# Output map of a hybrid encoder layer: seven block products with sums, or plain quarters with the feed-forward sums made per token tile

## Chip, cores and metric

One core of a Trainium2 chip runs the whole kernel. The metric is the device time of one execution in microseconds (us). The engines are PE (TensorE; PEld is its weight load), DVE (VectorE), ACT (ScalarE), POOL (GpSimd) and SP (SyncE, which issues most DMAs here).

## What is computed

One encoder layer on 1024 tokens of width 1024, all in float32, and a final norm:

```python
u = rms_norm(h, norm_mix[l])
proj = u @ w_in[l]
...
merged = jax.nn.sigmoid(g_pool) * y_pool + jax.nn.sigmoid(g_attn) * y_attn
h = h + merged @ w_out[l]
u = rms_norm(h, norm_ffn[l])
h = h + (jax.nn.silu(u @ w_ffn_gate[l]) * (u @ w_ffn_up[l])) @ w_ffn_down[l]
...
return rms_norm(h, norm_final)
```

`y_pool` and `y_attn` are two token mixers (pooling windows, and windowed attention), each followed by a map to width 1024, which the text calls a branch. `w_out` is the output map; gate, up and down have an inner width of 2816.

## The kernel before

**Arithmetic.** A float32 operand is split into two parts that PE takes (type fp32r): `hi` is ACT's cast of it, and `lo` is operand minus `hi`, made on DVE or POOL (`split`, L81). A product of two operands is three matmuls: hi by hi, hi by lo, lo by hi. A matmul covers 128 rows of the contraction and 512 columns.

**Seven products for eight.** Most maps are done by a scheme that cuts both operands in 2 x 2 blocks and computes seven block products in place of eight, from sums and differences of blocks. For gate and up the blocks of the activations are A11, A12 (first 512 tokens, first and second half of the width) and A21, A22 (last 512 tokens), and the sums are S1 = A21 + A22, S2 = S1 - A11, S3 = A11 - A21, S4 = A12 - S2. Products P1 and P2 need A11 and A12 alone; P5 needs S1, P6 S2, P7 S3, P3 S4, P4 A22 (`A_OF`, L126). The weight differences are made on POOL (`less`, L140).

**Weights.** All weight chunks come through one queue in the order of use (`specs`, `ahead`, `weights`): a 512 KB load into one of four `raw` tiles, then a split into one of four `whi` and one of four `wlo` tiles. A chunk is 12 matmuls of PE work.

**Stages around the change.** (1) The branch of the attention is mapped, gated and added to `merged`, first for token half 0, then for half 1 (`branch_step`, L687; its operand comes back from `a_dram` through `load_branch`, L564, into `a_hi`, `a_lo`). `merged` is kept transposed, [width, tokens], in two halves. (2) The output map `merged @ w_out` runs in the seven-product scheme (`operands_of`, L751; `block_products`, L809; `wo_done`, L909). Its P1 and P2 need only token half 0 and stand between the two branch halves; P5, P7, P6, P3, P4 follow half 1. Sums of `merged` blocks are made on DVE, weight differences on POOL, and results are added to rows `o`, which hold x. (3) The second norm takes rows tile by tile (`second_norm`, L885), and `finish` (L892) transposes a tile on PE (`tp`) and writes it to `merged`, whose place is free by then; for the first 512 tokens it also makes A11 and A12. (4) The first products of gate and up run (P1 and P2 of the first four column pairs), and meanwhile `u_block` (L970) makes A22, S1, S2, S3, S4 one after the other over 512 tokens, with the sums of S2 and S4 on POOL. Then gate and up continue to the end, and the down map follows.

**Order.** A scheduler puts each engine's instructions in an order when the program is built, so the order on an engine is not the order of the code. Each engine, and the SP queue of DMA issues, then works strictly in that order. Tiles of a pool that is opened after another was released may lie in the same memory, and then wait for its last users.

Of the kernel before, what the change touches and what calls it, by code (L numbers as in the profile page):

```python
# [8 lines left out]
F32 = mybir.dt.float32  # L9
# [5 lines left out]
P = 128  # L15
# [39 lines left out]
def encoder_kernel(ctx, tc, x, norm_mix, w_in, w_pool_group, pool_scale, sink, w_pool_branch,  # L55
# [788 lines left out]
    for name in ("A11", "A12"):  # L844
        combos[name] = tuple(first.tile([P, 4, HALF], F32R, name="%s_%s" % (name, s)) for s in ("hi", "lo"))
    op = tc.alloc_tile_pool(name="op", bufs=1)
    gain2 = const.tile([P, D], F32, tag="gain", bufs=1, name="gain_ffn")
    nc.scalar.dma_start(out=gain2, in_=norm_ffn[0:1, :].partition_broadcast(P))
    WO_ORDER = ("P1", "P2", "P5", "P7", "P6", "P3", "P4")
    NO = KT // 2  # L850
    _, wo_operands = operands_of(w_out, (range(NO), range(NO, KT)), NO,
                                 lambda i, r, k: merged[r][:, NO * i + k], [op],
                                 lambda prod, k: nc.vector if WO_POOL[prod] <= k else nc.gpsimd)

    def queue_wo(products):
# [36 lines left out]
    def finish():  # L892

        u2, t = pend.pop(0)
        ts = slice((t % 4) * P, (t % 4 + 1) * P)

        def emit(b, pv):
            m = merged[t // 4][:, 4 * b:4 * b + 4, ts]
            nc.scalar.copy(out=m, in_=pv)
            if t < 4:  # L900
                hi, lo = combos["A1%d" % (b + 1)]
                if LO_POOL[b]:
                    split(m, hi[:, :, ts], lo[:, :, ts], eng=nc.gpsimd)
                else:
                    split(pv, hi[:, :, ts], lo[:, :, ts])

        transposed(u2, emit)

    def wo_done(prod, t, ps):  # L909
        if prod == "P1":  # L910
            nc.scalar.copy(out=p1[t], in_=ps)
        elif prod == "P2":
            nc.scalar.copy(out=p2[t], in_=ps)
        elif prod == "P5":
            add_to(4 + t, 1, ps)
            add_to(t, 1, ps)
        elif prod == "P7":
            add_to(4 + t, 1, ps)
        elif prod == "P6":
# [11 lines left out]
    def wo_after(prod, t):  # L931
        if prod == "P4":
            finish()
            if t + U2_BUFS < NT // 2:
                second_norm(t + U2_BUFS)
# [292 lines left out]
```

## Time and profile before

| what | us |
|---|---|
| median of 3 runs (lowest to highest) | 1240.76 (1240.11 to 1240.97) |
| the profiled execution's own time | 1242.44 |
| span of the profile, first to last instruction | 1240.7 |
| PE busy | 1173.0 |
| DVE busy | 869.3 |
| POOL busy | 648.4 |
| ACT busy | 552.9 |

The profiled execution took 1.7 us more than the median and 1.7 us more than its span. Matmuls are pipelined: the end of one overlaps the start of the next, so the pace is read from the distance between starts. The granted clock (PEclk) is the share of full TensorE speed in a stretch. A wait is put down to the instruction whose end released it.

### The profile page before, as it was taken

To read this page: it belongs to the slowest core of one execution; us is meant where nothing else is said; L and a number is where in the kernel's file an instruction comes from. 1 tells how busy PE (TensorE), PEld (TensorE's weight loads), DVE (VectorE), ACT (ScalarE), POOL (GpSimd) and SP (SyncE) were. 2 spreads that over 40 slices of the span, in tenths; PEclk is the share of its full clock that TensorE was granted. 3 is DMA by queue.
4 is the path that set the end of the run, shared out by engine and by line. 5 is a ranking of instruction groups with operands and counts; after the bars stand their busy time and mean duration, and the time that the engine had idled before them with its cause. 6 is when DMAs were issued, how large, how long until landed. Compare 5 with 4: busy or idle time off the path is not lost.

```text
span 1240.7 us, 15495 instructions
## 1 busy us (share of the span) xinstructions
PE 1173.0 (95%) x5236; PEld 955.4 (77%) x5236; DVE 869.3 (70%) x1257; ACT 552.9 (45%) x1064; POOL 648.4 (52%) x531
## 2 busy tenths in 40 slices
PE   7899999999999998798699999999999999999996
PEld 5688888887778885576488888888888878887775
DVE  6954785757899656996996555665555675789974
ACT  6633354536677552357433333333333344443453
POOL 5833453344545638957765454654445623179530
PEclk9999999999899999799899999999999999999998
DMA  6343133126421654624144223232233358876362
GB/s 204 111 133 122 60 110 119 53 86 215 139 80 46 214 161 143 233 96 160 34 143 130 77 78 117 90 116 94 77 110 102 110 195 297 300 251 238 118 212 110
DMA packets 112337, 170.10 MB, mean 137 GB/s; under 512 B 7617, under 2 KB 63937, under 8 KB 112258
## 3 DMA queue, kind: packets, MB, share of 16 engines
q1 hardware_dynamic: 104338, 142.64, 35.3%
q0 software_dynamic: 6480, 21.24, 4.8%
q10 hardware_dynamic: 1440, 5.24, 1.1%
q8 instruction: 41, 0.67, 0.2%
q14 instruction: 38, 0.31, 0.1%
HBM read 128.99 MB, written 40.11 MB: 136 GB/s over the span
## 4 chain that ended last, share of the span: by engine, by line
PE 77%; DVE 14%; issue 3%; DMA 2%; POOL 2%; ACT 1%; SPq 0%; POOLq 0%; DVEq 0%; ACTq 0%
PE dn L820 17%; PE Y L179 16%; PE X L179 15%; PE Z L179 13%; PE W L179 8%; DVE wlo L84 2%; DVE o L870 2%; DVE al L84 1%; PE br L211 1%; PE br L210 1%; PE br L212 1%; DVE S_lo L84 1%; PE pt L657 1%; PE pv L670 1%; PE pv L671 1%
## 5 line engine op out<-in xcount | busy, mean ns | idle before, releaser
L83 ACT CAST whi<-raw 128x512 fp32r<-128x512 f32 x344 | 212.1, 620 | 392.9 <-PE Y L179 86.2
L84 DVE TENSOR_TENSOR wlo<-raw,whi 128x512 fp32r<-128x512 f32 x304 | 267.6, 889 | 73.7 <-ACT whi L83 73.0
L140 POOL TENSOR_TENSOR raw<-raw 128x512 f32<-128x512 f32 x140 | 196.6, 1406 | 217.5 <-DVE wlo L84 188.8
L820 PE MATMUL dn<-wlo,ah 128*128 128x512 f32 x420 | 167.8, 400 | 11.2 <-DVE wlo L84 11.0
L820 PE MATMUL dn<-whi,ah 128*128 128x512 f32 x420 | 159.6, 397 | 8.5 <-ACT ah L83 5.3
L820 PE MATMUL dn<-whi,al 128*128 128x512 f32 x420 | 162.4, 397 | 1.7 <-DVE al L84 1.7
L179 PE MATMUL X<-S_lo,whi 128*128 128x512 f32 x280 | 109.9, 393 | 4.1 <-DVE S_lo L84 4.0
L179 PE MATMUL X<-S_hi,whi 128*128 128x512 f32 x280 | 109.9, 392 | 2.7 <-ACT whi L83 2.7
L179 PE MATMUL X<-S_hi,wlo 128*128 128x512 f32 x280 | 109.4, 391 | 0.0
L820 PEld LDWEIGHTS dn<-wlo,ah 128*128 128x128 f32 x420 | 80.9, 193 | 31.6 <-DVE wlo L84 14.3
L820 PEld LDWEIGHTS dn<-whi,ah 128*128 128x128 f32 x420 | 80.2, 191 | 28.0 <-ACT ah L83 7.1
L820 PEld LDWEIGHTS dn<-whi,al 128*128 128x128 f32 x420 | 80.7, 192 | 19.3 <-DVE al L84 2.6
L84 DVE TENSOR_TENSOR al<-ab,ah 128x512 fp32r<-128x512 f32 x69 | 68.1, 987 | 31.1 <-ACT ah L83 30.8
L83 ACT CAST ah<-ab 128x512 fp32r<-128x512 f32 x69 | 42.7, 618 | 78.2 <-PE dn L820 76.5
L179 PE MATMUL Z<-A_hi,whi 128*128 128x512 f32 x176 | 70.0, 399 | 1.9 <-ACT A_hi L83 1.9
L179 PE MATMUL Z<-a,whi 128*128 128x512 f32 (+1 forms) x240 | 70.2, 377 | 0.3 <-ACT a L83 0.3
L179 PE MATMUL Z<-A_lo,whi 128*128 128x512 f32 x176 | 70.0, 398 | 0.0
L179 PE MATMUL Z<-A_hi,wlo 128*128 128x512 f32 x176 | 69.6, 396 | 0.0
L84 POOL TENSOR_TENSOR wlo<-raw,whi 128x512 fp32r<-128x512 f32 x40 | 56.8, 1425 | 23.2 <-ACT whi L83 20.0
L179 PEld LDWEIGHTS X<-S_lo,whi 128*128 128x128 f32 x280 | 52.7, 188 | 16.7 <-DVE S_lo L84 5.2
L179 PEld LDWEIGHTS X<-S_hi,whi 128*128 128x128 f32 x280 | 52.6, 188 | 15.1 <-ACT whi L83 3.3
L647 POOL TENSOR_SCALAR s<-s,den 128x384 f32<-128x384 f32 (+1 forms) x32 | 38.7, 1219 | 46.7 <-DVE den L645 27.5
(262 smaller groups left out, 2759.5 us busy)
## 6 DMA issues: line engine op xcount, KB each, us to landing
raw<-in_w_ffn_down_dram SPq DMA_DIRECT2D x45, 512.0 KB, 5.5
ab<-act_dram SPq DMA_DIRECT2D x31, 512.0 KB, 5.5
raw<-in_w_in_dram SPq DMA_DIRECT2D x26, 512.0 KB, 3.9
raw<-in_w_ffn_gate_dram SPq DMA_DIRECT2D x22, 512.0 KB, 4.1
raw<-in_w_ffn_up_dram SPq DMA_DIRECT2D x22, 512.0 KB, 3.8
act_dram<-sums POOLq DMA_DIRECT2D x44, 256.0 KB, 2.8
raw<-in_w_out_dram SPq DMA_DIRECT2D x18, 512.0 KB, 4.4
sg<-g_dram SPq DMA_DIRECT2D x32, 256.0 KB, 3.3
```

The source lines that it names most:

```text
L83: ins = nc.scalar.copy(out=hi, in_=src)
L84: (eng or nc.vector).tensor_tensor(out=lo, in0=src, in1=as32(hi), op=ALU.subtract)
L140: nc.gpsimd.tensor_tensor(out=out, in0=x0, in1=x1, op=ALU.subtract)
L179: nc.tensor.matmul(ps, wt[:, c], at[:, k, cols], start=opening and k == 0 and i == 0, stop=k == 3 and i == 2, skip_group_check=not opening)
L210: nc.tensor.matmul(ps, wh, xh, start=first, stop=False)
L211: nc.tensor.matmul(ps, wh, xl, start=False, stop=False)
L212: nc.tensor.matmul(ps, wl, xh, start=False, stop=last)
L647: (nc.gpsimd if i in POOL_HEADS else nc.vector).tensor_scalar(out=s[:, i, :W], in0=s[:, i, :W], scalar1=den[:, i:i + 1], scalar2=None, op0 ...
L657: nc.tensor.transpose(out=ps[:, i * P:(i + 1) * P], in_=s[:, i, jj * P:(jj + 1) * P], identity=ident)
L670: nc.tensor.matmul(ps, v, pt[jj][0], start=jj == 0, stop=False)
L820: nc.tensor.matmul(ps[t], at[:, ts], wt, start=opening and k == 0 and e == 0, stop=k == nk - 1 and e == 2, skip_group_check=not opening)
L870: (eng or nc.vector).tensor_tensor(out=o[t][:, half_of(c)], in0=src, in1=o[t][:, half_of(c)], op=ALU.add)
```

## The change

**What it does.** The output map is computed in plain quarters: token half by output half, eight contraction chunks each (`wo_product`), with 384 matmuls instead of 336. `merged` is split once per half into `m_hi`, `m_lo` (`split_merged`: half 0 beside branch half 1, half 1 after it). The weight chunks of `w_out` need no differences, and all quarters come after both branch halves. A quarter's last three chunks (`WO_TAIL`) are held back and run row by row, so that rows finish one after the other. The tiles of the first 512 tokens are normed and transposed beside the third quarter (`first_half`). For the last 512 tokens, `emit_sums` makes A22, S1, S2, S3 of one 128-token tile directly behind its transposes, all sums on DVE, in the memory of the split of `merged`; S4 alone remains a block over 512 tokens (`last_block`), also on DVE. The `lo` parts of the first gate and up chunks and of all `w_out` chunks move from POOL to DVE. By the instruction orders POOL has 58 instructions fewer and the DVE count falls by 6. Loads of `w_out` go from 18 to 16. Up to the output map a line of the changed kernel has a number 4 lower than before (L84 is L80).

```diff
+    def split_merged(half):
+        for j in range(KT):
+            split(merged[half][:, j], *[m[:, j] for m in m_split[half]])
...
+        def emit_sums(b, pv):
+
+            a11 = merged[0][:, :4, ts]
+            a21, s = [merged[1][:, 4 * i:4 * i + 4, ts] for i in range(2)]
+            if b == 0:
+                nc.scalar.copy(out=a21, in_=pv)
+                return
+            nc.vector.tensor_tensor(out=s, in0=pv, in1=a21, op=ALU.add)
+            split(pv, *part("A22"))
+            split(s, *part("S1"))
+            nc.vector.tensor_tensor(out=s, in0=s, in1=a11, op=ALU.subtract)
+            split(s, *part("S2"))
+            nc.vector.tensor_tensor(out=a21, in0=a11, in1=a21, op=ALU.subtract)
+            split(a21, *part("S3"))
...
-    wo_products(WO_ORDER[:2])
     while pool_steps:
         branch_step()
     brs[0].release()
     early = tc.alloc_tile_pool(name="early", bufs=1, side="right")
+    open_split()
+    split_merged(1)
...
+    def wo_product(half, c, beside):
+
+        ps = [bank("wo%d" % t) for t in range(4)]
+        hi, lo = m_split[half]
+
+        def accumulate(k, t, w):
+            ts = slice(t * P, (t + 1) * P)
+            for e, (at, wt) in enumerate(((hi, w[0]), (lo, w[0]), (hi, w[1]))):
+                nc.tensor.matmul(ps[t], at[:, k, ts], wt, start=k == 0 and e == 0, stop=k == KT - 1 and e == 2)
+
+        for k in range(KT - WO_TAIL):
+            w = weights()
+            for t in range(4):
+                accumulate(k, t, w)
+            ahead(1)
+            beside(k)
+        tail = [weights() for _ in range(WO_TAIL)]
+        for t in range(4):
+            for i in range(WO_TAIL):
+                accumulate(KT - WO_TAIL + i, t, tail[i])
+            row = 4 * half + t
+            if row not in o:
+                o[row] = ot.tile([P, D], F32, tag="o", bufs=4, name="o")
+                nc.sync.dma_start(out=o[row], in_=x[row * P:(row + 1) * P, :])
+            add_to(row, c, ps[t])
+            square(row, c, ot)
+            if c and t < U2_BUFS:
+                second_norm(row)
+        ahead(WO_TAIL)
...
-        if unit[2] == 1 and not late_pools:
-            open_late()
-            u_block("A22")
-            u_block("S1")
-            made |= set(("A22", "S1"))
-        if name not in made:
-            u_block(name)
-            made.add(name)
+        if (unit, prod) == f_seq[4 * EARLY + 2]:
+            last_block()
```

**SP queue, end of the attention.** `at` tiles are stored to `a_dram`, `sg` are gate loads, and `raw<-a_dram` are the two parts of the operand of branch half 1. Before:

```order
L679 DMA a_dram_70<-at_4138 128x2x128
L574 DMA sg_4240<-g_dram_67 128x512
L763 DMA raw_4378<-in_w_out_dram 128x2x512
L574 DMA sg_4265<-g_dram_67 128x512
L679 DMA a_dram_70<-at_4193 128x2x128
L574 DMA sg_4476<-g_dram_67 128x512
L100 DMA raw_4424<-in_w_attn_branch_dram 128x4x256
L574 DMA sg_4497<-g_dram_67 128x512
L574 DMA sg_4520<-g_dram_67 128x512
L100 DMA raw_4458<-in_w_attn_branch_dram 128x4x256
L574 DMA sg_4541<-g_dram_67 128x512
L568 DMA raw_4468<-a_dram_70 128x2x512
```

With the change:

```order
L564 DMA raw_4298<-a_dram_70 128x2x512
L570 DMA sg_4215<-g_dram_67 128x512
L675 DMA a_dram_70<-at_4138 128x2x128
L570 DMA sg_4238<-g_dram_67 128x512
L570 DMA sg_4259<-g_dram_67 128x512
L570 DMA sg_4306<-g_dram_67 128x512
L675 DMA a_dram_70<-at_4193 128x2x128
L564 DMA raw_4302<-a_dram_70 128x2x512
```

The last store (`at_4193`) moves behind one more gate load, the third after the store before it, and the second part of the operand is loaded directly behind that store.

**DVE, the same place.** `al` and `m_lo` are lo parts of `merged`, `a_lo` that of the operand of branch half 1; each `sg` is the product with a gate. Before:

```order
L711 TENSOR_TENSOR sg_4240<-br_4242,sg_4240 128x512
L84 TENSOR_TENSOR al_4317<-merged_2675,ah_4316 128x512
L84 TENSOR_TENSOR wlo_4289<-raw_4282,whi_4288 128x512
L711 TENSOR_TENSOR sg_4265<-br_4267,sg_4265 128x512
L84 TENSOR_TENSOR wlo_4321<-raw_4282,whi_4320 128x512
L84 TENSOR_TENSOR al_4339<-merged_2675,ah_4338 128x512
```

With the change:

```order
L80 TENSOR_TENSOR m_lo_4214<-merged_2675,m_hi_4213 128x512 x3
L707 TENSOR_TENSOR sg_4238<-br_4240,sg_4238 128x512
L80 TENSOR_TENSOR m_lo_4214<-merged_2675,m_hi_4213 128x512 x3
L80 TENSOR_TENSOR wlo_4279<-raw_4276,whi_4278 128x512
L707 TENSOR_TENSOR sg_4259<-br_4261,sg_4259 128x512
L80 TENSOR_TENSOR a_lo_3997<-raw_4302,a_hi_3996 128x2x512
```

The second `a_lo` of branch half 1 now stands behind six `m_lo`, and its load has no products of the output map beside it.

**DVE, behind the second norm.** Before, the sums over 512 tokens of S1 (L977) and S3 (L982), and their `lo` parts:

```order
L977 TENSOR_TENSOR merged_2676<-merged_2676 128x512
L84 TENSOR_TENSOR S1_lo_5487<-merged_2676,S1_hi_5486 128x512
L84 TENSOR_TENSOR wlo_5561<-raw_5555,whi_5560 128x512
L982 TENSOR_TENSOR merged_2676<-merged_2675,merged_2676 128x512
L84 TENSOR_TENSOR S3_lo_5491<-merged_2676,S3_hi_5490 128x512
L84 TENSOR_TENSOR S1_lo_5487<-merged_2676,S1_hi_5486 128x512
L84 TENSOR_TENSOR wlo_5584<-raw_5578,whi_5583 128x512
```

With the change, for the last token tiles (L933, L936, L938 are the sums of a tile; each `wlo` is of a weight chunk):

```order
L933 TENSOR_TENSOR merged_2676<-tp_5395,merged_2676 128x4x128
L80 TENSOR_TENSOR A22_5250<-tp_5353,A22_5250 128x4x128
L80 TENSOR_TENSOR S1_5251<-merged_2676,S1_5251 128x4x128
L80 TENSOR_TENSOR wlo_5459<-raw_5456,whi_5458 128x512
L80 TENSOR_TENSOR S2_5252<-merged_2676,S2_5252 128x4x128
L80 TENSOR_TENSOR S3_5253<-merged_2676,S3_5253 128x4x128
L80 TENSOR_TENSOR wlo_5483<-raw_5477,whi_5482 128x512
L938 TENSOR_TENSOR merged_2676<-merged_2675,merged_2676 128x4x128
L80 TENSOR_TENSOR A22_5250<-tp_5395,A22_5250 128x4x128
L936 TENSOR_TENSOR merged_2676<-merged_2676,merged_2675 128x4x128
L80 TENSOR_TENSOR S1_5251<-merged_2676,S1_5251 128x4x128
```

The sums start with the first transposed tile instead of after the last, and the last S1 part, which the first P5 product needs, comes behind the sums of the three tiles before it.

## Rows read from the trace of the kernel before

**Rows 1.** The page: span and busy time.

```profile
span 1240.7 us, 15495 instructions
PE 1173.0 (95%) x5236; PEld 955.4 (77%) x5236; DVE 869.3 (70%) x1257; ACT 552.9 (45%) x1064; POOL 648.4 (52%) x531
```

**Rows 2.** Windows: length, busy (count) of PE, PEld, DVE, ACT, POOL; PEclk, DMA share, GB/s.

```profile
482.50:523.00 40.50, 27.98 (x97) 20.81 (x97) 40.40 (x33) 15.09 (x30) 33.96 (x22) 0.83 0.55 208
523.00:562.00 39.00, 36.24 (x157) 29.08 (x157) 36.52 (x48) 15.66 (x35) 26.02 (x19) 0.96 0.27 89
562.00:570.50 8.50, 3.75 (x26) 2.94 (x26) 7.60 (x11) 7.84 (x18) 5.47 (x6) 1.00 0.67 243
570.50:594.60 24.10, 21.37 (x97) 17.09 (x97) 14.03 (x16) 16.41 (x32) 16.17 (x13) 0.93 0.40 123
594.60:622.00 27.40, 19.68 (x68) 14.51 (x69) 27.40 (x23) 12.20 (x22) 22.43 (x14) 0.88 0.05 17
```

**Rows 3.** Waits of PE, 482.5 to 622 us: total, times, longest.

```profile
PE dn L820 <- DVE wlo L84: 5.2, 1, 5.2
PE X L179 <- DVE S_lo L84: 4.0, 2, 2.7
```

**Rows 4.** Timeline of PE: start, duration, instruction, idle before.

```profile
438.13 0.39 PE L820 MATMUL dn<-whi,ah 128*128 128x512 f32 x1
...
459.91 0.39 PE L210 MATMUL br<-a_hi,whi 128*128 128x512 f32 x1
...
495.15 0.80 PE L820 MATMUL dn<-whi,ah 128*128 128x512 f32 x1 [2.80 <-ACT ah L83]
...
497.45 0.63 PE L820 MATMUL dn<-wlo,ah 128*128 128x512 f32 x1
497.88 0.63 PE L820 MATMUL dn<-whi,ah 128*128 128x512 f32 x1
...
567.07 1.20 PE L239 MATMUL tp<-ident,u 128*128 128x128 f32 x9 [0.81 <-ACT merged L899]
...
619.11 0.78 PE L179 MATMUL W<-S_lo,whi 128*128 128x512 f32 x1
```

**Rows 5.** Timeline of DVE and POOL near 595 us.

```profile
593.86 0.68 DVE L982 TENSOR_TENSOR merged<-merged 128x512 f32<-128x512 f32 x1
594.46 0.68 DVE L977 TENSOR_TENSOR merged<-merged 128x512 f32<-128x512 f32 x1
595.07 1.78 DVE L84 TENSOR_TENSOR S_lo<-merged,S_hi 128x512 fp32r<-128x512 f32 x1
...
594.48 1.82 POOL L140 TENSOR_TENSOR raw<-raw 128x512 f32<-128x512 f32 x1 [2.29 <-DMA raw<-in_w_ffn_up_dram]
```

**Rows 6.** Groups, 482 to 700 us: xcount | busy us, mean ns | idle before.

```profile
L84 DVE TENSOR_TENSOR S_lo<-merged,S_hi 128x512 fp32r<-128x512 f32 x16 | 20.0, 1291 | 0.0
L889 DVE SCALAR_TENSOR_TENSOR u<-o,rstd,gain_ffn 128x1024 f32<-128x1024 f32 x8 | 14.3, 1804 | 2.5 <-POOL rstd L882 2.5
```

**Rows 7.** Timeline of the SP queue: a gate load of branch half 1.

```profile
432.22 0.33 SPq L574 DMA_DIRECT2D sg<-g_dram  x1
```

**Rows 8.** DMA issues: count, KB each, median us to landing.

```profile
raw<-a_dram SPq DMA_DIRECT2D x4, 512.0 KB, 4.0
a_dram<-at SPq DMA_DIRECT2D x16, 128.0 KB, 1.8
```

**Rows 9.** Groups, 438 to 482 us.

```profile
L84 DVE TENSOR_TENSOR wlo<-raw,whi 128x512 fp32r<-128x512 f32 x10 | 8.2, 839 | 1.0 <-ACT whi L83 1.0
L711 DVE TENSOR_TENSOR sg<-br,sg 128x512 f32<-128x512 f32 x7 | 4.8, 690 | 8.7 <-PE br L212 7.5 <-issue 1.3
L84 DVE TENSOR_TENSOR a_lo<-raw,a_hi 128x1024 fp32r<-128x1024 f32 x2 | 2.5, 1226 | 7.7 <-ACT a_hi L83 7.7
L83 ACT CAST a_hi<-raw 128x1024 fp32r<-128x1024 f32 x2 | 2.1, 1050 | 4.4 <-DMA raw<-a_dram 4.4
```

**Rows 10.** The page, costliest groups: weight differences on POOL.

```profile
L140 POOL TENSOR_TENSOR raw<-raw 128x512 f32<-128x512 f32 x140 | 196.6, 1406 | 217.5 <-DVE wlo L84 188.8
```

More of the change, by code (lines that the diff above doesn't have):

```diff
@@ L895, in finish, with part @@
         ts = slice((t % 4) * P, (t % 4 + 1) * P)
+        def part(name):
+            hi, lo = combos[name]
+            return hi[:, :, ts], lo[:, :, ts]
         def emit(b, pv):
-            m = merged[t // 4][:, 4 * b:4 * b + 4, ts]
+            m = merged[0][:, 4 * b:4 * b + 4, ts]
             nc.scalar.copy(out=m, in_=pv)
[L900 to L905, printed above, removed]
@@ L931, in wo_after @@
[L931 to L935, printed above, removed]
-        elif t < U2_BUFS:
-            second_norm(t)
+            if LO_POOL[b]:
+                split(m, *part("A1%d" % (b + 1)), eng=nc.gpsimd)
+            else:
+                split(pv, *part("A1%d" % (b + 1)))
+        def emit_sums(b, pv):
[11 more added lines that the diff above has]
+            split(a21, *part("S3"))
@@ L945, in encoder_kernel @@
     f_seq = [(("f", m_, j), p) for m_, j, p in f_seq]
[L946 to L953 removed]
+    queue_products(f_seq, lambda u: ((w_g, w_u)[u[1]], 2 * u[2] * P), f_kinds)
     while pool_steps:
@@ L957, in encoder_kernel @@
     early = tc.alloc_tile_pool(name="early", bufs=1, side="right")
+    open_split()
+    split_merged(1)
     ot = tc.alloc_tile_pool(name="ot", bufs=1)
-    for t in range(NT):
-        o.append(ot.tile([P, D], F32, tag="o", bufs=NT, name="o"))
-        nc.sync.dma_start(out=o[t], in_=x[t * P:(t + 1) * P, :])
     ssq = ot.tile([P, 2, NT], F32, name="ssq2")
-    for t in range(NT // 2):
-        add_to(t, 0, p2[t], nc.gpsimd)
-        square(t, 0, ot)
-    wo_products(WO_ORDER[2:])
-    for t in range(U2_BUFS):
-        second_norm(4 + t)
@@ new lines, in first_half, with last_block @@
+    def first_half(k):
+        if k < NT // 2:
+            finish()
+            if k + U2_BUFS < NT // 2:
+                second_norm(k + U2_BUFS)
+    for half in range(2):
+        for c in range(2):
+            wo_product(half, c, first_half if (half, c) == (1, 0) else lambda k: None)
+    for half, names in enumerate((("A22", "S1"), ("S2", "S3"))):
+        for name in names:
+            in_place_of_split(half, name)
+    def last_block():
+        for k in range(4):
+            hi, lo = (t[:, k] for t in combos["S4"])
+            s = merged[1][:, 4 + k]
+            nc.vector.tensor_tensor(out=s, in0=merged[0][:, 4 + k], in1=s, op=ALU.subtract)
@@ L1067, in open_late @@
         ot.release()
-        op.release()
         second = tc.alloc_tile_pool(name="second", bufs=1)
-        for name in ("S1", "S2", "S3", "S4", "A22"):
-            combos[name] = tuple(second.tile([P, 4, HALF], F32R, name="%s_%s" % (name, s)) for s in ("hi", "lo"))
+        combos["S4"] = tuple(second.tile([P, 4, HALF], F32R, name="S4_%s" % s) for s in ("hi", "lo"))
         late_pools.extend((second, tc.alloc_tile_pool(name="ff", bufs=1)))
@@ L1113, in sums_of @@
             spill(name, j, out)
-    made = set(("A11", "A12"))
     for i, (unit, prod) in enumerate(f_seq):
```

87 lines of the change are left out of this document (27 added, 60 removed).

## Prediction

> **What bounds the kernel now.** The page comes first: PE is busy 1173.0 of 1240.7 us, DVE 869.3, POOL 648.4 [rows 1]. So PE sets the end, and the question is where its 67.7 idle us lie and where it runs slowly. The view by window answers the first part. From 482.5 us (end of the branch) to 622 us (first products of gate and up that need sums) PE is busy 27.98 + 36.24 + 3.75 + 21.37 + 19.68 = 109.0 of 139.5 us; 30.5 us are idle, while DVE is busy all the time at both ends of the stretch (40.40 of 40.50 and 27.40 of 27.40) and POOL for 33.96 and 22.43 [rows 2]. The waits of PE name the releasers: DVE and ACT, with parts of weights and of sums [rows 3]. The timeline gives the second part. Between 438.13 and 459.91 us 96 matmuls start 0.227 us apart; after a wait, as at 495.15, they start 0.43 us apart and last 0.63 us, the pace of the lower clock, 1.2 GHz in place of 2.4 [rows 4]. From 495.15 to 619.11 I count 56 such matmuls, in six runs, each soon after a wait; the granted clock of the windows with the longest waits is 0.83 and 0.88 [rows 2, 4]. They cost 56 x 0.20 = 11.2 us. Of what PE loses in this stretch, 30.5 + 11.2 = 41.7 us, the change can get back all or part, since nothing in it remains as it was.
>
> **What goes.** The operands of P5, P7, P6, P3 and P4, made one chunk ahead from sums on DVE and differences on POOL, are gone; `w_out` chunks are loaded and split only. With them go the waits from 482.5 to 562 us. The transposes of the first 512 tokens move beside the third quarter, those of the last 512 beside the first products of gate and up, so PE has other work between them. Removed: 41.7 us.
>
> **What is added on PE.** 384 matmuls for 336: 48 x 0.227 = 10.9 us, all on the path. The 64 transposes stay.
>
> **What hides the rest.** In the quarters PE eats a chunk in 12 x 0.227 = 2.7 us. A chunk needs one cast and one `wlo` (0.84 us on DVE [rows 9]) and half a load; the adds, squares, stores and norms of a quarter are spread over 21.8 us. The casts of `m_hi`, the 16 `m_lo` and the `lo` parts that leave POOL are priced at nothing where PE works on ready operands; their cover is the branch (22 us) for half 0 and two quarters (43 us) for half 1. POOL is left with powers and a few `lo` parts. The x loads (four at first, four more when rows are free) and the `h_dram` stores sit on the SP queue between `w_out` loads, and eight chunks are loaded or split ahead, 21.8 us of cover.
>
> **New wait 1, at 438 us.** Before, the products P1 and P2 of the output map, 21.8 us, stood between the branch halves and hid the return of the attention's last part. Now half 1 follows at once, and its seventh matmul needs the second part of its operand at 438.13 + 7 x 0.23 = 439.7 us. The last store to `a_dram` now stands on SP behind a gate load that was issued at 432.22 [rows 7], so it goes at 432.6, lands 1.8 later, and the part lands 4.0 after that [rows 8]: 438.4. Cast and `lo`, 1.05 and 1.23 us [rows 9], end at 440.7: a wait of 1.0 us. But DVE has six `m_lo`, a `wlo` and two gate products ahead of that `lo`, and the memory of `m_hi` is that of the stored tile, so they start after the store has landed, at 434.4 + 0.6 = 435.0: 7 x 0.84 + 2 x 0.69 = 7.3 us [rows 9], then 1.23, which ends at 443.5 and makes a wait of 3.8. If each of the seven met POOL's gate sums and took 1.78 us, as a `lo` part does beside POOL [rows 5], the wait would be 10.7. I take 4, since 0.84 is the mean beside the same POOL work; 1.0 and 10.7 are the ends.
>
> **New wait 2, behind the second norm.** From the first gate product to the first product with S1, PE has 96 matmuls and 32 transposes: 96 x 0.227 + 32 x 1.20 / 9 = 26.0 us [rows 4]. By the order of instructions DVE has in that time 24 short instructions with both inputs in SBUF (sums, `lo` parts, weights), 9 that read PSUM and 3 of the norm; up to the last part of S4 17 more, and one that reads PSUM, against three product pairs, 3 x 5.45 = 16.3 us. Alone, DVE starts one every 0.60 us, also with two SBUF inputs; beside a POOL subtraction the same kind takes 1.78 [rows 5]. With a mean m for these 41, and 1.80 for a norm [rows 6], the wait is 24m + 9 x 0.60 + 3 x 1.80 - 26.0 + 17m + 0.6 - 16.3 = 41m - 30.9. At m = 0.60 it is nothing. In the last window POOL was busy for 22.43 of 27.40 us, 0.82 [rows 2], and the mean of a `lo` part of a sum was 1.29 [rows 6], 0.61 above its 0.68 alone. Now POOL has only ten weight differences there, 10 x 1.41 us [rows 10] in some 42 us, 0.33. So m = 0.60 + 0.61 x 0.33 / 0.82 = 0.85, and the wait is 4 us. The ends are 0 and, at 1.29, 22.
>
> The Trainium skill, SBUF — State Buffer, "Who interferes with whom", states that a VectorE instruction with two SBUF inputs and a GpSimd instruction that reads SBUF exclude each other for a whole instruction. The trace agrees with the direction (0.68 alone, 1.78 beside POOL [rows 5]). By that rule each of the ten differences would hold DVE up for its full 1.41 us: 41 x 0.60 + 14.1 - 30.9 = 7.8 us, and the forecast would be 1224, inside its own range, so this is no rival.
>
> **New wait 3, the clock.** A wait of some us is followed by 56 / 6, about nine, slow matmuls [rows 4], 1.9 us. I take one such run.
>
> **Sum.** -41.7 + 10.9 + 4 + 4 + 2 = -20.8 us. The profiled execution took 1242.44 us, of which 1.7 lie outside the span; it would come to 1221.6. Its time is 1.7 above the median, 1240.76, on which the forecast is **1220.0**.
>
> **The rivals.** (A) *Nothing new waits*, beyond the 1.0 us of the load: -41.7 + 10.9 + 1.0 = -29.8, 1211. For it: DVE alone keeps ahead of PE, and POOL may do its differences early. Against it: the order of DVE puts the S1 part of the last tile behind nearly all sums of the others. (B) *VectorE half blocked behind the second norm*: m = 1.29 as now gives 22 in place of 4, 1238; m = 1.1 gives 14, 1230. For it: the same kinds of instruction had that mean in the trace. Against it: half of the POOL work of that window, the sums of S2 and S4 and weight parts, is gone. (C) *Slower*: the same place, but every one of the 41 loses to POOL and takes 1.78: 41 x 1.78 - 30.9 = 42 us, 1258. It decides from 41m - 30.9 = 30.8 - 6, m = 1.36, just above the mean now. For it, POOL's ten differences would have to be spread so that each instruction meets one; against it, ten cannot meet 41 unless each is stretched. The rule on exclusion above would make it likelier only with more POOL work than there is. (D) *The quarters do not run at full pace*: a wait for weights at each of the 32 chunks, 0.65 us each, takes back the 20.8 us, about the same time as before. For it: PE was idle for 40.50 - 27.98 = 12.5 us in the first window of the output map [rows 2]; against it: its operands there were sums and differences, which are gone.
>
> **How the numbers follow.** The forecast's case, 1214 to 1228, takes new wait 1 between 1 and 8 us and wait 2 up to 10: 0.67. A, below 1214: 0.11. B, 1228 to 1238: 0.13. C: 0.06. D: 0.03. A measurement tells 0.2%, 2.5 us, from no change. Faster: 0.67 + 0.11 + 0.13 = 0.91; same: D, 0.03; slower: C, 0.06. The range 1210 to 1233 takes in A and the nearer half of B and leaves out some 0.17.
>
> **What would show it.** Right: PE's idle time from the end of the branch to the S4 products under 13 us, against 30.5; 384 matmuls of the output map 0.227 us apart with a granted clock near 1.00; a wait of 1 to 8 us some seven matmuls into branch half 1, on `a_lo`; a mean of S1 and S3 parts on DVE under 1.0 us; PE waiting on S parts for 0 to 10 us. Wrong: waits on `whi` or `wlo` inside the quarters, waits of transposes on `u`, S parts above 1.3 us, or a clock below 0.9 in the quarters.

## The result and the profile after

| what | before, us | after, us |
|---|---|---|
| median (lowest to highest), same chip | 1240.43 (1237.14 to 1240.97) | 1207.78 (1206.62 to 1211.03) |
| ratio of the medians, 95% interval | | 0.9746, 0.9721 to 0.9772 |
| the profiled execution's own time | 1242.44 | 1207.96 |
| PE waits from 430 to 640 us | 30.5 | 3.3 |
| first branch product with attention weights to first product of the down map | 600.60 | 571.03 |
| first to last product of the down map | 218.81 | 215.57 |

The change is worth 32.65 us. The forecast was 20.8 us less, 1220.0, and its range began at 1210: the direction was right, the gain larger than the range allowed. The last two rows of the table are starts of PE's instructions in its timeline, 409.88, 1010.48 and 1229.29 us before, 408.21, 979.24 and 1194.81 after. The first of these stretches holds everything that the change touches: before it and behind it the traces of the two kernels have the same instructions in the same order on every engine. It is called *the stretch* below.

The page of the changed kernel, span and busy time (before: [rows 1]):

```profile
span 1206.2 us, 15486 instructions
PE 1167.2 (97%) x5284; PEld 955.4 (79%) x5284; DVE 834.1 (69%) x1251; ACT 543.1 (45%) x1044; POOL 563.8 (47%) x473
```

PE has 48 matmuls more and is busy for 5.8 us less, mainly since none of its work in the stretch runs at the lower pace any more. The view by window, with the columns of [rows 2], shows it for branch half 1 and what is around it, the four quarters, the first products of gate and up, and the first ones that need sums:

```profile
438.00:465.00 27.00, 26.15 (x111) 20.15 (x110) 27.00 (x31) 11.74 (x21) 15.64 (x9) 1.00 0.62 210
465.00:553.00 88.00, 88.00 (x410) 73.21 (x409) 45.02 (x66) 39.59 (x81) 11.37 (x11) 1.00 0.48 170
553.00:578.00 25.00, 24.70 (x121) 20.32 (x120) 25.00 (x37) 17.98 (x33) 10.73 (x8) 1.00 0.52 162
578.00:605.00 27.00, 25.97 (x113) 20.89 (x113) 24.99 (x32) 9.96 (x18) 11.41 (x9) 1.00 0.27 86
```

In the quarters PE has no gap in 88 us and DVE only half a load (45.02 of 88.00). Behind the norm DVE is full (25.00 of 25.00), and yet PE stands idle for 0.30 us there and for 1.03 us in the next window. The granted clock is 1.00 in all four, where [rows 2] has 0.83, 0.96, 1.00, 0.93 and 0.88 for the windows of before. These are all of PE's waits between 430 and 640 us (total, times, longest), against the 30.5 us of which [rows 3] shows two. `W`, `X`, `Y` and `Z` are results of gate and up products, `br` those of the branch; `S` stands for the parts of S1, S2 and S3, whose `hi` comes from ACT and whose `lo` from DVE:

```profile
PE W L175 <- ACT S L79: 1.0, 1, 1.0
PE W L175 <- DVE wlo L80: 0.8, 1, 0.8
PE X L175 <- DVE wlo L80: 0.5, 1, 0.5
PE br L206 <- ACT a_hi L79: 0.4, 1, 0.4
PE X L175 <- DVE S L80: 0.3, 1, 0.3
PE br L207 <- DVE a_lo L80: 0.3, 1, 0.3
```

The two `br` lines, 0.7 us, are the prediction's New wait 1. The two `S` lines, 1.3 us, are New wait 2. The two `wlo` lines come at 610 and 619 us, behind the first round of sums. No wait was followed by matmuls at the lower pace, so New wait 3 did not come. In place of 10 us that is 2.0, or 3.3 with the weights.

### The profile page after: what moved, and what is told of

It is laid out like the page before. It is cut to its first block, busy times and chain, and to the rows that moved or that the text cites. A ratio compares the mean times of both kernels' runs of the same rounds, so it can differ in the third digit from the quotient of the medians.

```text
span 1206.2 us, 15486 instructions
## 1 busy us (share of the span) xinstructions
PE 1167.2 (97%) x5284; PEld 955.4 (79%) x5284; DVE 834.1 (69%) x1251; ACT 543.1 (45%) x1044; POOL 563.8 (47%) x473
## 4 chain that ended last, share of the span: by engine, by line
PE 83%; DVE 10%; issue 2%; DMA 2%; POOL 1%; ACT 1%; SPq 0%; POOLq 0%; DVEq 0%; ACTq 0%
PE dn L816 16%; PE Y L175 15%; PE X L175 15%; PE Z L175 13%; PE W L175 8%; PE wo L969 7%; DVE wlo L80 2%; PE br L208 2%; PE br L207 2%; PE br L206 2%; PE pt L653 1%; DMA xt<-in_x_dram 1%; PE pv L667 1%; PE pv L666 1%; DVE S L80 1%
## 5 line engine op out<-in xcount | busy, mean ns | idle before, releaser
L80 DVE TENSOR_TENSOR wlo<-raw,whi 128x512 fp32r<-128x512 f32 x336 | 295.7, 888 | 106.1 <-ACT whi L79 101.0
L816 PE MATMUL dn<-wlo,ah 128*128 128x512 f32 x308 | 120.5, 392 | 4.2 <-DVE wlo L80 4.2
L816 PE MATMUL dn<-whi,al 128*128 128x512 f32 x308 | 118.3, 389 | 0.0
L816 PE MATMUL dn<-whi,ah 128*128 128x512 f32 x308 | 116.1, 390 | 1.0 <-ACT ah L79 1.0
L80 DVE TENSOR_TENSOR al<-ab,ah 128x512 fp32r<-128x512 f32 x69 | 67.0, 972 | 27.1 <-ACT ah L79 27.0
L175 PE MATMUL X<-S_hi,whi 128*128 128x512 f32 x192 | 75.6, 394 | 0.0
L175 PE MATMUL X<-S_lo,whi 128*128 128x512 f32 x192 | 75.5, 393 | 0.1
L175 PE MATMUL X<-S_hi,wlo 128*128 128x512 f32 x192 | 75.4, 393 | 0.0
L816 PEld LDWEIGHTS dn<-wlo,ah 128*128 128x128 f32 x308 | 57.8, 188 | 18.9 <-DVE wlo L80 7.1
L175 PE MATMUL W<-S,whi 128*128 128x512 f32 x176 | 54.6, 391 | 1.0 <-ACT S L79 1.0
L175 PE MATMUL X<-S,whi 128*128 128x512 f32 x176 | 54.5, 390 | 0.3 <-DVE S L80 0.3
```

The costliest lines, as they stand in the source:

```text
L80: (eng or nc.vector).tensor_tensor(out=lo, in0=src, in1=as32(hi), op=ALU.subtract)
L175: nc.tensor.matmul(ps, wt[:, c], at[:, k, cols], start=opening and k == 0 and i == 0, stop=k == 3 and i == 2, skip_group_check=not opening)
L816: nc.tensor.matmul(ps[t], at[:, ts], wt, start=opening and k == 0 and e == 0, stop=k == nk - 1 and e == 2, skip_group_check=not opening)
```

## The experiments

All times of the stretch and of the down map in one table, from one trace of each run. The kernel before was timed beside each group of runs, and the ratios are against it: its medians there were 1241.94 (e2 to e4), 1241.73 (e5 to e8), 1241.28 (e9, e10) and 1242.95 us (e11, e12). e1 is a single execution of 1248.12 us; e8 was timed twice, the others four or five times.

| run | stretch, us | down map, us | median, us | ratio, 95% interval |
|---|---|---|---|---|
| before | 600.60 | 218.81 | 1240.43 | |
| e1 before again | 601.08 | 225.25 | | |
| after | 571.03 | 215.57 | 1207.78 | 0.9746, 0.9721 to 0.9772 |
| e5 after again | 571.06 | 215.22 | 1210.86 | 0.9735, 0.9705 to 0.9766 |
| e11 after, third time | 570.84 | 218.91 | 1210.90 | 0.9730, 0.9705 to 0.9755 |
| e2 sums in blocks | 583.70 | 218.70 | 1220.90 | 0.9821, 0.9778 to 0.9865 |
| e3 sums on POOL | 575.13 | 217.25 | 1217.99 | 0.9794, 0.9755 to 0.9834 |
| e4 late operand first | 576.94 | 215.97 | 1217.36 | 0.9796, 0.9757 to 0.9836 |
| e6 weight parts on POOL | 576.19 | 218.33 | 1215.95 | 0.9779, 0.9750 to 0.9808 |
| e7 differences on DVE | 569.95 | 218.56 | 1209.40 | 0.9736, 0.9698 to 0.9774 |
| e8 48 matmuls left out | 561.19 | 223.27 | 1204.15 | 0.9682, 0.9631 to 0.9733 |
| e9 down map's sums on DVE | 570.46 | 214.41 | 1206.54 | 0.9716, 0.9692 to 0.9740 |
| e10 e7 and e9 together | 568.10 | 220.63 | 1205.82 | 0.9721, 0.9696 to 0.9745 |
| e12 e10 again, beside e11 | 568.06 | 214.28 | 1205.01 | 0.9682, 0.9658 to 0.9707 |

The stretch repeats to 0.5 us (600.60, 601.08; 571.03, 571.06, 570.84; 568.10, 568.06), while the down map scatters by 11 us. So the experiments are read by the stretch, and their medians stand beside it.

### e1 and e5: what is scatter

Edits: none. The kernel before and the changed kernel, each traced again.

> The kernel before, unchanged, for a second trace. The instructions up to the branch and those of the down map stand in the same order on every engine in both kernels, yet the changed kernel was 1.8 us faster up to its first branch product (146.6 against 148.3 us) and 3.2 us faster from the first to the last product of the down map (215.6 against 218.8 us). If these 5 us belong to the execution that was profiled, this trace has the start nearer 146.6, the down map nearer 215.6, and the stretch from the first branch product with attention weights (409.88) to the first product of the down map (1010.48) still 600.6 +-1 us. If they belong to the kernel, the start is again about 148.3 and the down map about 218.8, with a wait of some 2.8 us and slow matmuls about 169 us into it.

> The changed kernel, unchanged, for a second trace and for times beside the other runs. So far the down map, whose instructions stand in the same order in all kernels, took 215.6 us (changed kernel), 216.0, 217.3, 218.7 (its variants), 218.8 and 225.3 us (two traces of before). If that is scatter of the execution, the stretch from the first branch product with attention weights to the first product of the down map is again 571.0 +-0.7 us, and the down map lies anywhere from 215.5 to 220; the time 1207 to 1214. If the change makes the down map faster, it is below 216.5 again and the time is 1206 to 1209.

The stretch came out as expected, 601.08 and 571.06: the change takes 29.9 us out of it (the mean of two less the mean of three). What the text on e1 calls the first branch product, at 146.6 and 148.3 us, is a product `gm` of the same helper; the branches come later. The start does belong to the execution: the first product of the pool branch on PE stands at 301.64 us in the first trace of before, at 300.81 in the second, at 299.87, 300.64 and 300.66 in the three of the changed kernel, and at 299.43 to 301.00 in its variants, which have the same order up to there. The down map of before was not nearer 215.6 but longer still, 225.25; that of the changed kernel was 215.22 and, in e11, 218.91. The long forms have one of two waits, and e1 has both. There PE waited 3.28 us for a weight chunk, and 120 us further on, behind the sums of P6, 3.87 us for the second part of another; in e11 it waited 2.78 us in that place, in e5 1.03 and 0.60. Timelines of PE (`dn` is the down map), of e1:

```profile
1064.99 0.51 PE L820 MATMUL dn<-whi,ah 128*128 128x512 f32 x1 [3.28 <-ACT whi L83]
1185.38 0.50 PE L820 MATMUL dn<-wlo,ah 128*128 128x512 f32 x1 [3.87 <-DVE wlo L84]
```

of e11:

```profile
1148.98 0.50 PE L816 MATMUL dn<-wlo,ah 128*128 128x512 f32 x1 [2.78 <-DVE wlo L80]
...
1150.04 0.63 PE L816 MATMUL dn<-wlo,ah 128*128 128x512 f32 x1
```

and of e5:

```profile
1143.38 0.50 PE L816 MATMUL dn<-wlo,ah 128*128 128x512 f32 x1 [1.03 <-DVE wlo L80]
1147.00 0.50 PE L816 MATMUL dn<-wlo,ah 128*128 128x512 f32 x1 [0.60 <-DVE wlo L80]
```

In e11 the wait of 2.78 us is followed by matmuls of 0.63 us, the pace of the lower clock; in e5 the waits of 1.03 and 0.60 are not. But the same wait can also pass without it, as in e2:

```profile
1162.83 0.51 PE L816 MATMUL dn<-wlo,ah 128*128 128x512 f32 x1 [2.78 <-DVE wlo L80]
...
1163.88 0.40 PE L816 MATMUL dn<-wlo,ah 128*128 128x512 f32 x1
```

Both forms occur with the changed kernel, so the 3.2 us between the two traces of the result are no gain of the change that this study shows. Whether the kernel before draws the long form more often cannot be told from two and three traces.

### e2: the quarters alone

The sums go back to blocks of four tiles behind the whole norm, S2 and S4 on POOL as before. The core of the edit:

```diff
-            nc.vector.tensor_tensor(out=s, in0=pv, in1=a21, op=ALU.add)
-            split(pv, *part("A22"))
-            split(s, *part("S1"))
...
+            nc.scalar.copy(out=merged[1][:, 4 * b:4 * b + 4, ts], in_=pv)
...
+            u_block("A22")
+            u_block("S1")
```

> The changed kernel with plain quarters, but the sums S1, S2, S3, S4 and A22 made as before: in blocks of four tiles of 512 columns behind the whole norm, S2 and S4 with their sums on GpSimd. Theory 'both parts pay': the waits on S parts and weights that the kernel before had in its first products with sums (2.7 + 1.3 + 2.7 + 3.8 us, and slow matmuls behind them) come back; slower than the changed kernel by 6 to 13 us, 1214 to 1221. Rival 'the quarters are all of it': sums in blocks are hidden as well as sums by token tile, since GpSimd is nearly empty and VectorE has less to do up to the last tile; 1207 to 1210.

Measured: 1220.90, and the stretch 12.7 us longer than the changed kernel's, at the long end of the first theory. The last two windows of the list above, now of e2:

```profile
553.00:578.00 25.00, 23.89 (x121) 19.54 (x120) 17.79 (x26) 17.77 (x34) 7.76 (x6) 1.00 0.60 179
578.00:605.00 27.00, 19.38 (x71) 14.23 (x69) 25.16 (x21) 10.81 (x19) 25.77 (x14) 0.81 0.13 39
```

And its longest groups of PE's waits from 430 to 640 us:

```profile
PE W L175 <- ACT whi L79: 4.6, 2, 2.4
PE Y L175 <- DVE act L1113: 2.5, 1, 2.5
PE W L175 <- DVE wlo L80: 2.4, 2, 2.0
```

In the first window DVE idles for 7.2 us; in the second POOL is busy for 25.77 of 27.00 us, PE does 71 instructions where it did 113, and the granted clock is 0.81. So what e2 keeps of the change (the quarters, the first tiles beside the third one, `lo` parts of the first chunks on DVE) takes 600.84 - 583.70 = 17.1 us out of the stretch, and the sums by token tile, on VectorE, another 12.7. e2 changes two things at once, when the sums are made and, for S2 and S4, on which engine; e3 below changes the engine alone, for 12 sums, and costs 4.1 us.

### e3 and e6: work back on POOL

In e3 the 12 sums that read SBUF alone go to POOL, in e6 second parts of weights of the first four gate and up units.

The first of e3's three lines, and the edit of e6:

```diff
-            nc.vector.tensor_tensor(out=s, in0=s, in1=a11, op=ALU.subtract)
+            nc.gpsimd.tensor_tensor(out=s, in0=s, in1=a11, op=ALU.subtract)
```

```diff
-    queue_products(f_seq, lambda u: ((w_g, w_u)[u[1]], 2 * u[2] * P), f_kinds)
+    queue_products(f_seq, lambda u: ((w_g, w_u)[u[1]], 2 * u[2] * P), f_kinds,
+                   lambda u: nc.gpsimd if u in f_kinds else None)
```

> The changed kernel with the 12 sums that read SBUF alone (S2 and S3 by token tile, S4 in four pieces) on GpSimd in place of VectorE. Theory 'cover': VectorE has 12 instructions fewer, the other 29 meet GpSimd more often; with the share of GpSimd at 0.71 the prediction's formula gives m = 1.13 and 29 x 1.13 - 30.9 + 12 x 0 = about the same wait as now, 1 to 3 us: 1206 to 1211. Rival 'VectorE alone is what makes it': each sum goes through a second queue and holds VectorE's next instruction, waits of 4 to 10 us on S parts: 1212 to 1218.

> The changed kernel with the removed setting F_POOL put back: the second parts of the weights of the first four gate and up units on GpSimd in place of VectorE (28 of them). Theory from the run with the sums on GpSimd: while both engines have work, each instruction of one makes the other wait (VectorE 1.77, GpSimd 1.74 us in turn there), so what VectorE sheds it loses again, and GpSimd's queue of differences and second parts (2 x 1.4 us or more per product against PE's 2.7) is late: slower by 3 to 10 us, 1211 to 1219. Rival, the prediction's formula: 25 VectorE instructions at up to 1.25 us need 31 us, so no wait: 1207 to 1210.

The number 28 in the second text is wrong: the setting acts on P1 and P2 of the four units alone, so eight second parts move. POOL of e6 from 500 to 640 us:

```profile
L80 POOL TENSOR_TENSOR wlo<-raw,whi 128x512 fp32r<-128x512 f32 x8 | 12.7, 1604 | 22.4 <-ACT whi L79 22.4
```

Measured: the stretch is 4.1 us longer in e3 and, with these eight, 5.2 us longer in e6; the medians are 1217.99 and 1215.95. In both cases the prediction's formula, which sees no harm, falls. In e3 it was right about the size that it computes. The groups of DVE from 552 to 590 us, of e3 (count, busy us, mean ns, idle before; busy counts the overlap of neighbours once):

```profile
L80 DVE TENSOR_TENSOR wlo<-raw,whi 128x512 fp32r<-128x512 f32 x11 | 14.4, 1313 | 0.7 <-ACT whi L79 0.7
L80 DVE TENSOR_TENSOR S<-merged,S 128x512 fp32r<-128x512 f32 x12 | 13.6, 1158 | 0.1
```

With the one `S_lo` of 1.562 us that makes a mean of (11 x 1.313 + 12 x 1.158 + 1.562) / 24 = 1.25 us, less the 0.08 us by which starts overlap 1.17, where the formula had 1.13. What it left out are the other queues. Of PE's two waits of 1.77 us, the one that ends at 579.61 goes back to POOL: the weight difference at 575.00 stood behind a sum at 573.30, and its cast and `wlo` (577.81) followed late. The one that ends at 573.24 goes back to ACT: its cast of the weights, at 572.57, stood behind a cast of A22 that had waited 1.29 us for a sum on DVE, and behind two casts of sums, while the last difference had been done at 569.87. The two engines move in step here. DVE of e3 around 575 us:

```profile
573.81 1.77 DVE L80 TENSOR_TENSOR wlo<-raw,whi 128x512 fp32r<-128x512 f32 x1
...
577.81 1.75 DVE L80 TENSOR_TENSOR wlo<-raw,whi 128x512 fp32r<-128x512 f32 x1
```

and POOL:

```profile
573.30 1.73 POOL L936 TENSOR_TENSOR merged<-merged 128x512 f32<-128x512 f32 x1
575.00 1.74 POOL L136 TENSOR_TENSOR raw<-raw 128x512 f32<-128x512 f32 x1
```

Each of these POOL instructions lasts 1.73 us and the DVE instruction that meets it 1.77, where the same form takes 0.68 alone. The Trainium skill, SBUF — State Buffer, "Who interferes with whom", states that a VectorE instruction with two SBUF inputs and a GpSimd instruction that reads SBUF exclude each other; the trace agrees (573.81 + 1.77 = 575.58, which is 0.55 us after POOL's end at 575.03). PE's waits in the stretch, of e3:

```profile
PE X L175 <- DVE wlo L80: 2.2, 2, 1.8
PE X L175 <- ACT whi L79: 1.8, 1, 1.8
```

and of e6:

```profile
PE X L175 <- ACT whi L79: 3.6, 1, 3.6
PE W L175 <- DVE wlo L80: 1.6, 2, 1.0
```

They are waits on weights, not on S parts as the rival of e3 had it (0.6 us in all on `S`). PE's waits are 2.8 and 3.4 us longer in all than in the changed kernel; the rest of the 4 and 5 us are matmuls at the lower pace behind them, eight in each, 1.6 us by their starts. The `whi` of e6, too, stood on ACT behind a cast that waited for a sum of DVE, one of 1.75 us beside POOL.

### e4: the late operand without its cover

Branch half 1 takes the contraction blocks of the late part first. The core of the edit:

```diff
-        ps = branch(held["w"], hi, lo, sl)
+        ps = branch(held["w"], hi, lo, sl, (2, 3, 0, 1) if b and half else (0, 1, 2, 3))
```

> The changed kernel, but the branch with the attention weights takes, for the second 512 tokens, the third and fourth contraction blocks first and the first and second last; nothing else. The operand that the prediction saw coming late is then the first that is needed. The prediction let it be covered by seven matmuls (1.6 us). Theory 'cover by order': the program takes the ready halves of the next output blocks ahead, about 29 matmuls instead of 7 stand before the late VectorE part, so its lateness was right and its cover wrong; without cover PE waits from 436.5 to about 440.3 and again to about 443.3, 5 to 7 us in all in place of 0.7, with perhaps 2 us of slow matmuls behind: 1212 to 1216. Rival 'the operand is simply not late': a wait of at most 2.3 us (0.7 + 1.6), 1208 to 1210.

Measured: 1217.36, and the branch (first to last of its products with attention weights) took 58.69 us in place of 52.12, so 6.6 us more (5.9 over the whole stretch). The timeline of PE, of the changed kernel:

```profile
436.46 0.39 PE L206 MATMUL br<-a_hi,whi 128*128 128x512 f32 x1
...
440.30 1.02 PE L206 MATMUL br<-a_hi,whi 128*128 128x512 f32 x3 [0.41 <-ACT a_hi L79]
...
443.43 0.50 PE L207 MATMUL br<-a_lo,whi 128*128 128x512 f32 x1 [0.30 <-DVE a_lo L80]
```

and of e4:

```profile
441.30 2.07 PE L206 MATMUL br<-a_hi,whi 128*128 128x512 f32 x4 [4.21 <-ACT a_hi L79]
444.15 0.79 PE L207 MATMUL br<-a_lo,whi 128*128 128x512 f32 x1 [0.78 <-DVE a_lo L80]
444.74 0.63 PE L208 MATMUL br<-a_hi,wlo 128*128 128x512 f32 x1
```

Half 1 starts at 436.46. In the changed kernel 14 matmuls stand ahead of the first one that needs the late `a_hi`, and 23 ahead of the first that needs the late `a_lo`, where the order of the code has 6 and 7: the program takes the ready blocks of the next output tiles ahead (three `hi` by `hi` in a row at 440.30). I had expected 29. Without them PE waits 4.21 + 0.78 us and then runs at the lower pace for the four matmuls at 441.30 and six single ones. The operand is late, as was forecast; it is the cover that was counted wrongly.

### e7: POOL emptied

```diff
-            nc.gpsimd.tensor_tensor(out=out, in0=x0, in1=x1, op=ALU.subtract)
+            on = nc.vector if unit[0] == "f" and unit[2] < 2 else nc.gpsimd
+            on.tensor_tensor(out=out, in0=x0, in1=x1, op=ALU.subtract)
```

> The changed kernel with the 16 weight differences of the first four gate and up units on VectorE in place of GpSimd, so that GpSimd has next to nothing to do behind the second norm. In the trace of the changed kernel five VectorE instructions there took 1.77 us and two 1.20 in place of 0.68, each beside such a difference. Theory 'an instruction on GpSimd costs VectorE 1.1 us, on VectorE itself 0.6': VectorE gains about 2 us up to the S4 parts, and the waits of 0.3 and 1.0 us on S parts shrink or go; the stretch comes to 569.5 to 571, the time to 0 to 1.5 us less. Rival 'GpSimd is a second engine all the same': VectorE, busy all the time there, is later by 5 x 0.6 us and more, and PE waits 2 to 5 us more on S parts and weights.

Measured: the stretch 569.95, of which the part from the first gate product to the down map is 424.2 us against 427.1 in the changed kernel; 1.8 us were lost again in the branch (53.93 us in place of 52.12), which did not come back in e10 and e12 (52.08, 52.04). The median, 1209.40, lies inside the range of the changed kernel's times. Groups of DVE from 552 to 590 us, first of the changed kernel:

```profile
L80 DVE TENSOR_TENSOR wlo<-raw,whi 128x512 fp32r<-128x512 f32 x12 | 10.4, 867 | 0.0
L80 DVE TENSOR_TENSOR S<-merged,S 128x512 fp32r<-128x512 f32 x12 | 9.6, 817 | 0.1
L936 DVE TENSOR_TENSOR merged<-merged 128x512 f32<-128x512 f32 x4 | 4.3, 1084 | 0.0
L938 DVE TENSOR_TENSOR merged<-merged 128x512 f32<-128x512 f32 x4 | 3.8, 961 | 0.0
L906 DVE SCALAR_TENSOR_TENSOR u<-o,rstd,gain_ffn 128x1024 f32<-128x1024 f32 x3 | 3.8, 1279 | 0.0
...
L1009 DVE TENSOR_TENSOR merged<-merged 128x512 f32<-128x512 f32 x4 | 2.5, 687 | 0.0
L80 DVE TENSOR_TENSOR S_lo<-merged,S_hi 128x512 fp32r<-128x512 f32 x2 | 1.3, 690 | 0.0
```

and POOL, in the same stretch:

```profile
L136 POOL TENSOR_TENSOR raw<-raw 128x512 f32<-128x512 f32 x8 | 12.5, 1567 | 12.3 <-DVE merged L936 4.2 <-DVE wlo L80 3.8 <-DMA raw<-in_w_ffn_gate_dram 2.6
```

then DVE of e7:

```profile
L80 DVE TENSOR_TENSOR wlo<-raw,whi 128x512 fp32r<-128x512 f32 x13 | 8.9, 683 | 0.6 <-ACT whi L79 0.6
L80 DVE TENSOR_TENSOR S<-merged,S 128x512 fp32r<-128x512 f32 x12 | 8.1, 682 | 0.0
L137 DVE TENSOR_TENSOR raw<-raw 128x512 f32<-128x512 f32 x8 | 5.5, 685 | 0.0
```

Without POOL beside them `wlo` and `S` take 0.68 us, and eight differences more find room on DVE. In the changed kernel the 38 short DVE instructions of those 38 us with two SBUF inputs (all rows shown but `u`) last, count times mean, 10.40 + 9.80 + 4.34 + 3.84 + 2.75 + 1.38 = 32.5 us, 6.5 more than 38 x 0.684. That is what eight POOL differences cost DVE, 0.82 us each; on DVE itself they cost 0.60 each, start to start. So DVE gains a little by the exchange, 0.2 us for each. PE gains 2.7 to 2.9 us behind the first gate product: the two waits on S parts and the two on `wlo` at 610 and 619 us are gone, and one of 1.0 us on `whi`, one matmul behind the place of the longer S wait, is new. By the starts 1.0 us is gained up to there and 1.8 at the two `wlo`.

### e8: the price of the 48 matmuls

Left out are the products of the first three chunks of each quarter with the second part of the weights.

```diff
+                if e == 2 and k < 3:
+                    continue
```

> The changed kernel without 48 of the 384 matmuls of the output map: in each quarter the products of the first three chunks with the second part of the weights are left out; casts, second parts and loads stay. It measures what the 48 matmuls that the change adds cost. Theory 'PE is the bound in the quarters': 48 x 0.227 = 10.9 us less, the stretch 571.0 becomes 560 +-1. Rival 'weights or splits set the pace': less than 8 us.

The stretch is 9.8 us shorter (561.19 against 570.98, the mean of three), 0.2 us less than the expected 560 +-1 allows. One wait is new, in the first quarter, on the second part of a weight chunk:

```profile
PE wo L971 <- DVE wlo L80: 0.7, 1, 0.7
```

So it is 10.5 us for 48 matmuls by PE alone. PE is the bound in the quarters, and the term of 10.9 us was sized well.

### e9 to e12: does it go further?

```diff
-            add_to(t, 1, s1[t], nc.gpsimd)
+            add_to(t, 1, s1[t])
```

This is e9, in the down map's P6. e10 and e12 have it and the edit of e7; e11 is the changed kernel beside e12.

> The changed kernel with one more thing moved to VectorE: in the down map the four sums of the first half of the rows behind P6, which stood on GpSimd beside eight of VectorE's. In the traces so far VectorE's sums there took up to 1.8 us each beside GpSimd's, and behind them PE waited for the second part of a weight chunk, either 1.0 + 0.6 us or once 2.8 us with six slow matmuls after it; which of the two differed from trace to trace with one order of instructions. Theory 'both engines on SBUF take turns': four more sums cost VectorE 4 x 0.60 = 2.4 us and give back about 1.1 us for each that no longer meets GpSimd; the wait there falls under 1.7 us and the down map takes 213.5 to 216 us, against 215.2 to 218.7 in the variants. Rival 'the sums on VectorE are what is late': the wait grows to 3 us or more, the down map takes 218 to 221 us.

> Both moves to VectorE together: the 16 weight differences of the first gate and up units and the four sums of the down map. If they add, the stretch from the branch to the down map takes 569.5 to 570.5 us, the down map 213.5 to 216 us, and the time is 1205 to 1209. If the down map's duration is scatter that these sums don't touch, it is again anywhere from 215 to 219 and the time 1207 to 1212.

> The changed kernel once more, beside the next one on the same chip: the stretch 571.0 +-0.5 us, the down map 215 to 220 by scatter, the time 1207 to 1211.

> The variant with the weight differences and the down map's four sums on VectorE once more, beside the changed kernel on the same chip. If the first trace's stretch of 568.1 us and a down map of about 214.5 us without a late weight load are the kernel's own, the time is 2 to 5 us under the changed kernel's, 1203 to 1207; if the gain was scatter, the two are within 1 us.

In e9 the wait behind P6 falls to 0.43 us and the down map takes 214.41 us, the shortest up to then. In e10 the two gains of the stretch and of P6 add (568.10, below the expected 569.5 since e7's loss in the branch did not return; a wait of 0.43 behind P6), but a late weight chunk (2.31 us on `whi`, and matmuls at the lower pace behind it) made its down map 220.63: the sums on DVE remove one cause of the scatter and not the other. In e12 that chunk was not late, and the down map took 214.28. PE's waits of e12 from 430 to 640 us are:

```profile
PE W L176 <- ACT whi L79: 1.0, 1, 1.0
PE br L207 <- ACT a_hi L79: 0.5, 1, 0.5
PE br L208 <- DVE a_lo L80: 0.3, 1, 0.3
```

Side by side on one chip the variant took 1205.01 us (1204.23 to 1205.14) and the changed kernel 1210.90 (1209.90 to 1211.74); no execution of the one overlaps one of the other, and the 5.9 us between them are a little more than the 2 to 5 expected. The variant beats both kernels. Against the changed one about 2.9 us lie in the stretch (568.08 against 570.98, means); in the one trace of each on that chip 4.6 us lie in the down map (214.28 against 218.91), which e10 shows is not always so.

## Why the prediction was right and wrong

**Right: what bounds, and what goes.** PE sets the end in both kernels, its waits between 482 and 622 us and the slow matmuls behind them were the loss, and the change takes them out. The removed 41.7 us were a little more: the stretch of the changed kernel less its waits, plus the waits of before and less the 10.5 us of e8, is 571.0 - 3.3 - 10.5 + 30.5 = 587.7, and 600.8 less that leaves 13.1 us for slow matmuls where 11.2 were counted. The trace of before agrees: 67 of its matmuls there start more than 0.30 us apart without a wait between, and cost 12.9 us above 0.227. The slow ones alone were not too few in the count: 49 last 0.55 us or more, against 56. What it left out are the first starts behind a wait, 0.50 to 0.60 us apart (495.15 to 495.75), and single ones of 0.32 to 0.34.

**Right: what is added.** The 48 matmuls cost 10.5 us (e8) against 10.9. The casts, `m_lo` and splits priced at nothing cost nothing: PE is busy for 88.00 of 88.00 us in the quarters.

**Wrong: New wait 1, 4 us forecast, 0.7 measured.** The failed step is "its seventh matmul needs the second part of its operand". The lateness was not overestimated: the forecast had `a_lo` done at 443.5 us, and it was done at 443.38 (its timeline row starts at 442.17 and lasts 1.21) in an execution that was 1.7 us ahead by then, so 1.6 us later than forecast. The first `m_lo` began 2.3 us later than forecast by that measure (at 435.64), and the nine instructions ahead of the `a_lo` took 0.7 us less. Of DVE, in the changed kernel:

```profile
442.17 1.21 DVE L80 TENSOR_TENSOR a_lo<-raw,a_hi 128x1024 fp32r<-128x1024 f32 x1
```

But 23 matmuls stood ahead of it on PE, and 14 ahead of the first that needs the late `a_hi`, not six. e4 took this cover away and the branch became 6.6 us longer, so the range of 1.0 to 10.7 was no exaggeration for an uncovered operand. (Its upper end is added up wrongly: 7 x 1.78 + 2 x 0.69 + 1.23 behind 435.0 gives a wait of 10.4.) The order of PE in the trace shows these matmuls; the prediction's seventh is that of the code.

**Wrong in size: New wait 2, 4 us forecast, 1.3 measured.** The term 41m - 30.9 took m = 0.85. The 38 instructions above have a mean of 32.5 / 38 = 0.86 us, less 0.08 us of overlap between starts 0.78; and a norm took 1.28 us where 1.80 was used. With both, 41 x 0.78 - 30.9 - 3 x 0.52 = -0.5, so no wait is left by the formula, and 0.3 + 1.0 us were measured. POOL's share was as forecast, 12.5 of 38 us, 0.33; what it cost DVE was less than in proportion to the window of before. The formula has a worse fault that the changed kernel hardly exposed: it counts DVE alone. Where POOL is given work again (e3, e6) PE waits for weights that the formula takes as ready, and whose parts were late on POOL's queue or on ACT's. In the changed kernel itself 1.3 us of such waits on `wlo` came, which no term had.

**Wrong: New wait 3, 2 us forecast, nothing measured.** It hung on the first two. The longest wait in the stretch is 1.01 us, and the granted clock is 1.00 in the four windows above.

**The rivals.** A, nothing new waits, 1211, came nearest: its -29.8 us is the stretch's -29.9. That the two meet so closely is in part luck: 1.9 us more went than A took out, and 0.4 less was added, while waits of 3.3 us came where A had 1.0. It was given 0.11, with the argument that the order of DVE puts the S1 part of the last tile behind nearly all sums of the others. It does, and DVE is full there, but the S1 part was only 0.3 us late. B and C need more POOL work than the changed kernel has; e3 and e6 put some back, and it cost 4 and 5 us, mostly by waits on weights and not by late S parts as B and C have it. D fell with PE's 88.00 of 88.00 busy us in the quarters.

**Outside the sum.** The medians differ by 32.65, 30.9 (e5) and 32.0 us (e11) where the stretch gives 29.9. Between the two traces of the result the rest is 1.7 us in the start and 3.2 in the down map, whose orders of instructions are the same in both kernels and whose durations scatter (215.2 to 225.3 us for the down map). That the other 1 to 3 us of the medians lie there too is likely, but no trace of those executions shows it. The prediction's range had no term for the scatter of stages that the change does not touch. With one of 2 to 3 us its lower end would have lain at 1207 to 1208, about where the median is.

## What to carry to other kernels

Before a late operand is priced as a wait, count in the built order how many ready instructions of *other* tiles stand ahead of the first one that needs it. When VectorE and GpSimd both work on SBUF, price an instruction on GpSimd by what it costs VectorE (0.82 us here, against 0.60 for doing it on VectorE) and look at the queues of GpSimd and ScalarE as well: near a point where PE has little cover, doing all of it on VectorE can be the faster split. Measure a change in the stretch that it touches, between two instructions of the bounding engine: that repeated to 0.5 us here, while the whole kernel varied by several.

## What the runs showed that was not expected

With the same order of instructions on every engine the down map took between 215.2 and 225.3 us. The difference is made of few events: a weight chunk late by 1.4 to 3.3 us (e2, e8, e1), or one wait of 2.8 us in place of 1.0 + 0.6 behind P6, often followed by a run of matmuls at the lower pace (13 rows of 0.58 to 0.63 us in e8, behind waits of 2.46 and 0.63). Often and not always: a wait of 2.76 to 2.79 us in the same place behind P6 was followed by six to eight matmuls at the lower pace in four traces (before, e6, e7, e11) and by none in two (e2, e8). What decides it these runs do not show. A wait of 1.77 us at 573.24 us in e3 was not followed by slow matmuls, and the next one of 1.77 us, at 579.61 with 0.62 us of waiting between them, was: single matmuls take 0.63 us from there to 582.60. Why a weight chunk is late in one execution and not in another stays open.
